# Both down products of a macaron encoder step by 7 products of half blocks

## The chip, the cores and the metric

One NeuronCore of a Trainium2 chip (trn2) runs one inference step of a streaming encoder in fp32 accuracy. The metric is the device time of an execution in microseconds.

## The reference

The kernel computes the whole layer for 16 meta tokens, 1024 prompt frames and 32 frames of a running stream (1072 tokens, 1024 channels). What the change touches is the half-step FFN at either end, with 2816 hidden channels:

```python
def half_ffn(x, g, w_gate, w_up, w_down):
    h = rmsnorm(x, g)
    return x + 0.5 * ((jax.nn.silu(h @ w_gate) * (h @ w_up)) @ w_down)

x = half_ffn(x, ffn1_norm[l], ffn1_w_gate[l], ffn1_w_up[l], ffn1_w_down[l])
h = rmsnorm(x, mix_norm[l])
... = jnp.split(h @ w_in[l], split_at, axis=-1)     # attention, HGRN2, gates, w_out
x = half_ffn(x, ffn2_norm[l], ffn2_w_gate[l], ffn2_w_up[l], ffn2_w_down[l])
y_prompt = rmsnorm(xp, final_norm)[:, N_META:]
```

FFN1 takes all 1072 tokens, FFN2 the 1056 without the meta tokens. Behind FFN1 the sums are normalised for the input projection; behind FFN2 they are normalised, transposed and written out.

## The kernel before, in words

Every fp32 matrix is held as two fp32r parts, `hi` (a copy rounded by ACT) and `lo` (the difference, made by DVE), both made by `split` (L202) or `weights` (L169); every product is three matmuls into one PSUM bank: hi by hi, hi by lo, lo by hi. Channels lie on the 128 partitions, tokens in the free dimension.

**The gate and up stage** (`Seven.unit`, L345) takes 256 hidden channels (two chunks of 128, a unit; 11 units, of which the first goes by `plain`) and the tokens in two halves `b` of two quarters each (`QW` = 268 columns in FFN1, `QW2` = 264 in FFN2). For each weight, gate then up, it forms sums S1 to S4 of half blocks on DVE and needs 7 products of half blocks for each `b` in place of 8; partial sums are kept in SBUF (`parts`) by ACT and added by DVE in `out`. `g` (silu(gate) times up) goes to `mid_dram` by the SP queue (`store`, L315).

**The down stage** (`Seven.down`, L421) is a plain product. It goes through 11 pairs of chunks: `prepare` loads and splits two 512 KB rows of the weight and two chunks of `mid_dram`; `multiply` takes three tiles of tokens (`TT`: 400, 384, 288; `TD`: 384, 384, 288), 8 output chunks and 2 x 3 matmuls each, in PSUM banks that rotate through all eight (`bank(rotate=True)`, L129), and DVE adds half of the sum to `acc` (L443), which was loaded with the residual. For the last two pairs PE's order is written out by hand (`PE.on`), so that `after` (the end of one tile) runs beside the products of the next.

- FFN1: `after1` writes `x1_dram` and calls `normalise` (L214): for each chunk ACT makes `xh` (L218) and DVE `xl` (L219), ACT the squares (L224, L227), POOL adds five of them and DVE three (L228); `finish` sums over the partitions on PE and takes the root. Then the input projection (`project_all`) begins with its weights.
- FFN2: `after2` takes the blocks of 128 tokens that are complete: 8 transposes into two banks, two squares with their sums on ACT (L1520), a root, a reciprocal, two scalings on DVE (L1528) and the write.

```python
for i, x in ((last - 1, 0), (last - 1, 1), (last, 0), (last - 1, 2), (last, 1), (last, 2)):
    multiply(i, *tiles[x])
    if i == last:
        after(*tiles[x])
```

## Time and profile before

| | us |
|---|---|
| runs | 2502.64, 2504.14, 2504.74 (median 2504.14) |
| profiled execution | 2504.92 |
| its span | 2503.1 |
| PE busy | 2449.8 (98%), 18972 matmuls |
| DVE, ACT, POOL busy | 1540.3 (62%), 891.9 (36%), 149.9 (6%) |
| DMA | 211.95 MB, 83 GB/s of HBM traffic over the span |

An engine's busy time is the sum over its instructions. Its share is an average over stages: gate and up of FFN1 end at 510.8 us, the first down product at 773.45; the second down product runs from 2226.8 to 2491.4. A wait of another engine matters only where PE, or the chain at the end, waits for it.

### The profile page before, as it was taken

The page shows a single profiled execution, that of the slowest core. Times are in us where ns is not written, and L with a number is a line of the kernel's source. Part 1 is how long each engine was busy: PE and PEld are TensorE (multiplying, and loading weights), DVE is VectorE, ACT ScalarE, POOL GpSimd, SP SyncE. Part 2 cuts the span into 40 slices and gives each one's busy share as a digit, 9 for nine tenths or more (in the row PEclk, how much of TensorE's full clock was granted, in tenths as well). Part 3 has the DMA queues.
Part 4 walks back from the last instruction along what each step waited for, and adds up shares of the span by engine and source line. Part 5 has one row for each costly group of instructions (what it writes and reads, how often), then busy time and mean ns, then how long its engine had stood idle before and what let it go on. Part 6 is the DMA issues. An engine that isn't in the chain of part 4 may idle for free. (4 is left out here: it accounts for less than half of the span.)

```text
span 2503.1 us, 46037 instructions
## 1 busy us (share of the span) xinstructions
PE 2449.8 (98%) x18972; PEld 2347.6 (94%) x18972; DVE 1540.3 (62%) x2862; ACT 891.9 (36%) x1783; POOL 149.9 (6%) x307
## 2 busy tenths in 40 slices
PE   6999999999999999999999999999899999999998
PEld 5999999999999998898888887999899999999998
DVE  5755555567776377764666665657855555557766
ACT  6433333421125233332454544323443333331112
POOL 1000000000003012121000000111000000000000
PEclk9999999999999999999999999999899999999999
DMA  7122222252313111111111222432222222253311
GB/s 202 56 87 71 88 71 88 79 201 95 104 43 114 51 44 48 56 52 50 52 44 44 56 61 79 170 108 82 92 78 69 86 78 77 92 184 103 100 57 77
DMA packets 231913, 211.95 MB, mean 85 GB/s; under 512 B 38214, under 2 KB 209478, under 8 KB 231702
## 3 DMA queue, kind: packets, MB, share of 16 engines
q1 hardware_dynamic: 231670, 209.00, 26.1%
q8 instruction: 149, 2.44, 0.4%
q14 instruction: 62, 0.51, 0.1%
q0 software_dynamic: 32, 0.00, 0.0%
HBM read 154.00 MB, written 54.97 MB: 83 GB/s over the span
## 5 line engine op out<-in xcount | busy, mean ns | idle before, releaser
L102 PE MATMUL ps_mm<-xh,whi 128*128 128x384 f32 (+2 forms) x952 | 317.8, 334 | 0.6 <-DVE raw L1194 0.6
L102 PE MATMUL ps_mm<-xh,wlo 128*128 128x384 f32 (+2 forms) x952 | 310.9, 327 | 0.0
L102 PE MATMUL ps_mm<-xl,whi 128*128 128x384 f32 (+2 forms) x952 | 310.6, 326 | 0.0
L186 ACT ACTIVATE whi<-raw 128x1024 fp32r<-128x1024 f32 x109 | 112.9, 1055 | 537.1 <-PE ps_z L102 346.3
L204 DVE TENSOR_TENSOR wlo<-raw,whi 128x1024 fp32r<-128x1024 f32 x80 | 76.7, 959 | 209.4 <-ACT whi L203 206.9
L102 PEld LDWEIGHTS ps_mm<-xh,whi 128*128 128x128 f32 x952 | 179.9, 189 | 9.1 <-issue 5.0
L443 DVE SCALAR_TENSOR_TENSOR acc<-ps_z,acc 128x384 f32<-128x384 f32 (+2 forms) x264 | 138.7, 525 | 71.5 <-PE ps_z L102 70.1
L102 PEld LDWEIGHTS ps_mm<-xl,whi 128*128 128x128 f32 x952 | 180.1, 189 | 1.1
L102 PEld LDWEIGHTS ps_mm<-xh,wlo 128*128 128x128 f32 x952 | 180.0, 189 | 0.4
L187 DVE TENSOR_TENSOR wlo<-raw,whi 128x1024 fp32r<-128x1024 f32 x109 | 133.1, 1238 | 26.7 <-ACT whi L186 24.4
L986 DVE TENSOR_TENSOR_SCAN left<-left,oneb 128x512 f32<-128x512 f32 (+6 forms) x112 | 107.4, 959 | 54.8 <-ACT left L118 54.3
L203 ACT ACTIVATE whi<-S 128x1024 fp32r<-128x1024 f32 x80 | 85.0, 1062 | 155.9 <-PE ps_z L102 145.2
L204 DVE TENSOR_TENSOR wlo<-S,whi 128x1024 fp32r<-128x1024 f32 x80 | 97.9, 1224 | 29.9 <-ACT whi L203 28.6
L102 PE MATMUL ps_z<-acc1s,whi 128*128 128x268 f32 (+1 forms) x480 | 106.0, 285 | 0.0
L102 PE MATMUL ps_z<-xl1s,whi 128*128 128x268 f32 (+1 forms) x368 | 105.1, 286 | 0.0
L102 PE MATMUL ps_z<-xh1s,wlo 128*128 128x268 f32 (+1 forms) x368 | 104.9, 285 | 0.0
L102 PE MATMUL ps_z<-xh1s,whi 128*128 128x268 f32 (+1 forms) x368 | 104.6, 284 | 0.0
L203 ACT ACTIVATE whi<-raw 128x1024 fp32r<-128x1024 f32 x80 | 67.7, 846 | 92.6 <-PE ps_z L102 92.6
L443 DVE SCALAR_TENSOR_TENSOR acc<-ps_mm,acc 128x384 f32<-128x384 f32 (+2 forms) x132 | 69.2, 524 | 35.8 <-PE ps_mm L102 33.8
L118 ACT ACTIVATE g<-g 128x268 f32<-128x268 f32 (+1 forms) x120 | 50.8, 423 | 87.3 <-DVE g L378 84.1
L102 PEld LDWEIGHTS ps_z<-acc1s,whi 128*128 128x128 f32 x480 | 80.0, 188 | 0.0
L988 DVE TENSOR_TENSOR aa<-aa,left 128x512 f32<-128x512 f32 (+6 forms) x112 | 61.5, 550 | 14.4 <-POOL left L982 0.5
(694 smaller groups left out, 7416.9 us busy)
## 6 DMA issues: line engine op xcount, KB each, us to landing
raw<-in_ffn_w_gate_dram SPq DMA_DIRECT2D x44, 512.0 KB, 3.6
raw<-in_ffn_w_up_dram SPq DMA_DIRECT2D x44, 512.0 KB, 3.6
raw<-in_ffn_w_down_dram SPq DMA_DIRECT2D x44, 512.0 KB, 4.2
raw<-in_w_in_dram SPq DMA_DIRECT2D x44, 512.0 KB, 3.7
mid_dram<-g SPq DMA_DIRECT2D x22, 536.0 KB, 2.7
g<-mid_dram SPq DMA_DIRECT2D x22, 536.0 KB, 3.6
mid_dram<-g SPq DMA_DIRECT2D x22, 528.0 KB, 2.7
g<-mid_dram SPq DMA_DIRECT2D x22, 528.0 KB, 4.1
```

Source lines behind the costliest of these rows:

```text
L102: return self.queue(nc.tensor.matmul(*args, **more))
L118: i = A.activation(out, in_, func, **more).ins
L186: A.activation(hi, raw, AF.Copy)
L187: V.tensor_tensor(lo, raw, hi.bitcast(F32), op=ALU.subtract)
L203: A.activation(dst_h, src, AF.Copy)
L204: V.tensor_tensor(dst_l, src, dst_h.bitcast(F32), op=ALU.subtract)
L443: V.scalar_tensor_tensor(acc[:, m, s], ps[:, :n], 0.5, acc[:, m, s], op0=ALU.mult, op1=ALU.add)
L986: V.tensor_tensor_scan(rev(st[:rows]), rev(st[:rows]), one, 1.0 if carry is None else carry[:rows], op0=ALU.mult, op1=ALU.mult)
L988: V.tensor_tensor(at[:rows, :n], at[:rows, :n], left[:rows, 513 - n:], op=ALU.mult)
```

## The change

The down products become products of half blocks too. A unit is 2 x 128 hidden channels; a position `mp` is 256 output channels; a half `b` is two quarters of tokens. For each of them 7 products stand in place of 8. The seven operands on the side of the tokens (`NAMES`) are formed in the gate stage, once per unit, as hi and lo, through two staging tiles (`st`, and the place of `R`), and are written to `mid_dram` by the POOL queue (`send`, one of them after every second step by `tick`). `home` reads them back on SP into the slots of `xh` and `xl` and extra places, three units in turn. `lanes` loads weights of two (unit, position) pairs, forms four sums of 256 columns and their hi and lo. A `Job` is a position with two lanes and both halves, in tiles of two PSUM banks (`pv`, two `pu`, `pf`); ACT copies the first product from `pv` to `pu` within PSUM, and DVE adds six results of 2 x 268 columns to `acc`, or ACT writes them where they are the first. p6 and p7 of a job run between p1 and p4 of the next. The last two units run half by half in tiles of one bank, and `after` follows each half, in PE's written order. `acc` is no longer loaded with the residual: it is added in eight pieces on the way (`add_residual`). In the last up unit the first half's seven products come before the second half's. `after1` takes the first 400 tokens after the first half, the other two tiles after the second; `after2` takes blocks 0 to 3, then 4 to 8, and its transposes use three banks.

```diff
-PLACES = ((0, 0, 0), (0, 0, 1), (1, 0, 0), (1, 0, 1), (1, 1, 0), (1, 1, 1), (0, 1, 0), (0, 1, 1))
+PLACES = ((0, 0, 0), (1, 0, 0), (1, 1, 0), (0, 1, 0), (0, 0, 1), (1, 0, 1), (1, 1, 1), (0, 1, 1))
+NAMES = ("B11", "T3", "B21", "T2", "T4", "T1", "B22")
...
+        def send(self, i, gs):
+            def part(c, th):
+                return gs[c][:, self.t0:].rearrange("p (b t n) -> p b t n", b=2, t=2)[:, :, th]
+            def away(name, v, left=None, right=None):
+                def work():
+                    if left is not None:
+                        V.tensor_tensor(v, left, right, op=ALU.subtract)
+                    x = NAMES.index(name)
+                    if x % 2:
+                        st = base.tile([P, 2, 2, self.qw], F32R, tag="R", name="st")
+                    else:
+                        st = self.pool.tile([P, 2, 2, self.qw], F32R, tag="st", name="st", bufs=1)
+                    split(st[:, 0], st[:, 1], v)
+                    nc.gpsimd.dma_start(self.mids[i, :, x], st.rearrange("p a b n -> p (a b) n").bitcast(F32))
+                self.later.append(work)
+            b11, b12, b21, b22 = (part(c, th) for c in range(2) for th in range(2))
+            away("B11", b11)
+            away("T1", b11, b12, b11)
+            away("B21", b21)
+            away("T3", b12, b22, b12)
+            away("B22", b22)
+            away("T2", b22, b22, b11)
+            away("T4", b21, b21, b22)
+        def tick(self):
+            self.groups += 1
+            if self.later and self.groups % 2:
+                self.later.pop(0)()
...
+            steps = first, second, third, fourth, fifth, sixth, seventh
+            if i == FC // 2 - 1 and not gate:
+                for b in range(2):
+                    for step in steps:
+                        step(b)
+            else:
+                for step in steps:
+                    for b in range(2):
+                        step(b)
+                    self.tick()
...
+        def home(self, i):
+            j = i % 3
+            tiles = [slots(tag, j, F32R, None, self.qw) for tag in ("xh", "xl")]
+            for tag, n in self.homes[j]:
+                tiles.append(self.pool.tile([P, 1, 4, self.qw], F32R, tag=tag, name=f"u_{tag}", bufs=n))
+            places = []
+            for t in tiles:
+                x, n = len(places), t.shape[1]
+                nc.sync.dma_start(t.bitcast(F32), self.mids[i, :, x:x + n])
+                places += [t[:, y] for y in range(n)]
+            return dict(zip(NAMES, places))
...
+            split(ah[:, 0], al[:, 0], a11)
+            split(ah[:, 1], al[:, 1], a12)
+            split(ah[:, 2], al[:, 2], a22)
+            s = self.tile("S", [P, 4, 2, P])
+            V.tensor_tensor(s[:, 2], a21, a22, op=ALU.add)
+            V.tensor_tensor(s[:, 1], s[:, 2], a11, op=ALU.subtract)
+            V.tensor_tensor(s[:, 0], a11, a21, op=ALU.subtract)
+            V.tensor_tensor(s[:, 3], a12, s[:, 1], op=ALU.subtract)
+            sh = wp.tile([P, 4, 2, P], F32R, tag="whi", name="whi")
+            sl = wp.tile([P, 4, 2, P], F32R, tag="wlo", name="wlo")
+            split(sh, sl, s)
...
+                def out(job, mh, th, ps):
+                    m = 2 * job.mp + mh
+                    if job.b is None:
+                        to = acc[m].rearrange("p (b t) n -> p b t n", b=2)[:, :, th]
+                    else:
+                        to = acc[m][:, 2 * job.b + th]
+                    if (m, th) in begun:
+                        V.scalar_tensor_tensor(to, job.at(ps), 0.5, to, op0=ALU.mult, op1=ALU.add)
+                    else:
+                        begun.add((m, th))
+                        A.activation(to, job.at(ps), AF.Copy, scale=0.5)
...
+                def p1(job):
+                    job.v = job.tile("pv")
+                    job.product(job.v, "A11", "B11", True)
+                    job.u = job.tile("pu")
+                    A.activation(job.at(job.u), job.at(job.v), AF.Copy)
+                def p2(job):
+                    job.f = job.tile("pf")
+                    job.product(job.f, "S3", "T3", True)
+                    job.out(1, 1, job.f)
+                def p3(job):
+                    job.product(job.v, "A12", "B21", False)
+                    job.out(0, 0, job.v)
+                def p4(job):
+                    job.product(job.u, "S2", "T2", False)
+                    job.out(1, 0, job.u)
+                def p5(job):
+                    job.product(job.f, "A22", "T4", False)
+                    job.out(1, 0, job.f)
+                def p6(job):
+                    job.product(job.u, "S1", "T1", False)
+                    job.out(1, 1, job.u)
+                def p7(job):
+                    job.product(job.u, "S4", "B22", False)
+                    job.out(0, 1, job.u)
+            def run(jobs):
+                before = None
+                for job in jobs:
+                    job.p1()
+                    if before:
+                        before.p6()
+                    job.p2()
+                    job.p3()
+                    if before:
+                        before.p7()
+                    job.p4()
+                    job.p5()
+                    before = job
+                before.p6()
+                before.p7()
...
+            def add_residual(m):
+                r = self.tile("s", [P, 4, qw])
+                nc.sync.dma_start(r.rearrange("p q n -> p (q n)"), resid[:, m, self.t0:])
+                V.tensor_tensor(acc[m], acc[m], r, op=ALU.add)
+            def steps():
+                units[0] = self.home(0)
+                W = self.lanes(w, ((0, 2), (0, 3)))
+                while self.later:
+                    self.later.pop(0)()
+                units[1] = self.home(1)
+                for l in range(2):
+                    yield Job(W, [(units[0], l)], 2 + l)
+                for s in range(1, last):
+                    for mp in ((0, 1) if s % 2 else (2, 3)):
+                        if mp % 2 == 0:
+                            units[s + 1] = self.home(s + 1)
+                        W = self.lanes(w, ((s - 1, mp), (s, mp)))
+                        if mp % 2 and s > 1:
+                            add_residual((s - 2) // 2 + (4 if s % 2 else 0))
+                        yield Job(W, [(units[s - 1], 0), (units[s], 1)], mp)
+            psum("pairs")
+            PE.on = True
+            run(steps())
+            psum("singles")
+            Ws = [self.lanes(w, ((last - 1, mp), (last, mp))) for mp in (2, 3)]
+            Ws.append(self.lanes(w, ((last, 0), (last, 1)),
+                                 [self.tile("raw2", [P, 3, 2, P], F32R) for _ in range(2)]))
             functions(final)
-            PE.on = True
-            for i, x in ((last - 1, 0), (last - 1, 1), (last, 0), (last - 1, 2), (last, 1), (last, 2)):
-                multiply(i, *tiles[x])
-                if i == last:
-                    after(*tiles[x])
-                elif x == 2:
-                    between()
+            for b in range(2):
+                jobs = [Job(Ws[x], [(units[last - 1], 0), (units[last], 1)], 2 + x, b) for x in range(2)]
+                jobs += [Job(Ws[2], [(units[last], l)], l, b) for l in range(2)]
+                run(jobs)
+                after(b)
+            between()
...
+        def after1(b):
+            if not fed:
+                fed.update(xh=big("xh", F32R), xl=big("xl", F32R), R=base.tile([P, T], F32, tag="R", name="R"))
+            flat = [a.rearrange("p q n -> p (q n)") for a in ff.acc]
+            for t0, n in TT[1:] if b else TT[:1]:
+                for m in range(KC):
+                    nc.sync.dma_start(x1_dram[:, m, t0:t0 + n], flat[m][:, t0:t0 + n])
+                normalise(pool, [a[:, t0:t0 + n] for a in flat], fed["xh"], fed["xl"], 1, fed["R"], t0, n)
...
-                    ps = bank(rotate=True)
+                    ps = bank(("mm", "mm", "tr")[rot[0] % 3])
+                    rot[0] += 1
                     for k in range(4):
-                        PE.transpose(ps[:r, k * P:(k + 1) * P], acc[:, 4 * hf + k, c0:c0 + r], ident)
+                        PE.transpose(ps[:r, k * P:(k + 1) * P], acc[4 * hf + k][:, c0 - N_META:c0 - N_META + r], ident)
                     A.activation(junk[:r], ps[:r], AF.Square, accum_out=ss[:r, hf:hf + 1])
```

The order of instructions at three places, before and after.

PE in FFN2, where the last two pairs of chunks are multiplied (before) and where the first half of the last two units ends (after). `cst` is the identity, `acc*` the sums that are transposed, `mid_*`, `whi`, `wlo` operands of the down product; a row `[waits DVE_49]` waits for DVE.

```order
L102 MATMUL ps_z<-mid_gb,raw_26076 128x384
L105 MATMUL ps_mm<-cst,acc_24091 128x128 [waits DMAHW1_49,DVE_49]
L105 MATMUL ps_mm<-cst,acc_24091 128x128 [waits DVE_49] x3
L105 MATMUL ps_z<-cst,acc_24091 128x128 [waits DVE_49] x4
L105 MATMUL ps_tr<-cst,acc_24091 128x128 x4
L105 MATMUL ps_z<-cst,acc_24091 128x128 x4
L105 MATMUL ps_o<-cst,acc_24091 128x128 x4
L105 MATMUL ps_z<-cst,acc_24091 128x128 x4
L102 MATMUL ps_mm<-mid_mh,whi 128x288 x2
L102 MATMUL ps_mm<-mid_mh,wlo 128x288
```

```order
L106 MATMUL ps_mm<-cst,acc1s 128x128 [waits DVE_49]
L106 MATMUL ps_mm<-cst,acc1s 128x128
L106 MATMUL ps_mm<-cst,acc2s 128x128 x2
L106 MATMUL ps_tr<-cst,acc0s 128x128 [waits DVE_49]
L106 MATMUL ps_tr<-cst,acc0s 128x128 x2
L106 MATMUL ps_tr<-cst,acc1s 128x128
L106 MATMUL ps_mm<-cst,acc1s 128x128 [waits DVE_49]
L106 MATMUL ps_mm<-cst,acc1s 128x128
L106 MATMUL ps_mm<-cst,acc2s 128x128 x2
L103 MATMUL ps_z<-xh0s,g 128x264 x3
L103 MATMUL ps_z<-xh1s,g 128x264 x3
```

Before, six transposed tiles follow each other in six banks and the products of the next tile come behind them. Now the tiles take `mm`, `mm` and `tr` in turn, each second half of a block waits for DVE, and the other half's first product stands behind all of them.

DVE at FFN1's end: `xl` is the low part of the projection's operand (three tensors by tile of tokens in the change), `acc*` the sums, `L443` and `L566` the results of products.

```order
L187 TENSOR_TENSOR wlo<-raw,whi 128x1024 [waits DMAHW0_49,Activation_49]
L443 SCALAR_TENSOR_TENSOR acc_5430<-ps_z,acc_5430 128x384 [waits PE_49]
L443 SCALAR_TENSOR_TENSOR acc_5430<-ps_o,acc_5430 128x384 [waits PE_49]
L219 SCALAR_TENSOR_TENSOR xl_5439<-acc_5430,gains,xh_5436 128x384 [waits Activation_49]
L443 SCALAR_TENSOR_TENSOR acc_5430<-ps_z,acc_5430 128x384 [waits PE_49]
L219 SCALAR_TENSOR_TENSOR xl_5439<-acc_5430,gains,xh_5436 128x384 [waits Activation_49]
L443 SCALAR_TENSOR_TENSOR acc_5430<-ps_mm,acc_5430 128x384 [waits PE_49]
L219 SCALAR_TENSOR_TENSOR xl_5439<-acc_5430,gains,xh_5436 128x384 [waits Activation_49]
L443 SCALAR_TENSOR_TENSOR acc_5430<-ps_z,acc_5430 128x384 [waits PE_49]
L219 SCALAR_TENSOR_TENSOR xl_5439<-acc_5430,gains,xh_5436 128x384 [waits Activation_49]
```

```order
L566 SCALAR_TENSOR_TENSOR acc2s<-ps_z,acc2s 128x268 [waits PE_49]
L566 SCALAR_TENSOR_TENSOR acc1s<-ps_z,acc1s 128x268 [waits PE_49]
L566 SCALAR_TENSOR_TENSOR acc2s<-ps_z,acc2s 128x268 [waits PE_49]
L566 SCALAR_TENSOR_TENSOR acc2s<-ps_o,acc2s 128x268 [waits DVE_49,PE_49]
L235 SCALAR_TENSOR_TENSOR xl_8259<-acc0s,gains,xh_8256 128x400 [waits PE_49,Activation_49]
L235 SCALAR_TENSOR_TENSOR xl_8259<-acc0s,gains,xh_8256 128x400 [waits Activation_49] x2
L235 SCALAR_TENSOR_TENSOR xl_8259<-acc1s,gains,xh_8256 128x400 [waits Activation_49] x3
L235 SCALAR_TENSOR_TENSOR xl_8259<-acc2s,gains,xh_8256 128x400 [waits Activation_49] x2
L566 SCALAR_TENSOR_TENSOR acc2s<-ps_z,acc2s 128x268 [waits PE_49]
L566 SCALAR_TENSOR_TENSOR acc0s<-ps_o,acc0s 128x268 [waits PE_49]
L566 SCALAR_TENSOR_TENSOR acc0s<-ps_z,acc0s 128x268 [waits PE_49]
L235 SCALAR_TENSOR_TENSOR xl_8261<-acc1s,gains,xh_8258 128x288 [waits Activation_49]
```

Before, one `xl` stands behind each result. Now the eight `xl` of the 400 tokens stand in a row between results of the second half; the first of them waits for PE, whose products read the same slot.

ACT where the down product of FFN1 begins: `pu<-pv` are the copies within PSUM, `acc*<-p*` first results of a position, `st<-g` the splits of operands that are sent to DRAM; `DMASW` is POOL's DMA queue.

```order
L186 ACTIVATE whi<-raw 128x1024 [waits DMAHW0_49,DVE_49,PE_49]
L186 ACTIVATE whi<-raw 128x1024 [waits DMAHW1_49,DVE_49,PE_49]
L203 ACTIVATE mid_xe_6104<-g 128x1072 [waits DMAHW6_49]
L203 ACTIVATE mid_s<-g 128x1072 [waits DMAHW7_49]
L186 ACTIVATE whi<-raw 128x1024 [waits DMAHW4_49,DVE_49,PE_49]
L186 ACTIVATE whi<-raw 128x1024 [waits DMAHW5_49,DVE_49,PE_49]
```

```order
L219 ACTIVATE st<-g 128x536 [waits DMASW7_49,DVE_49,Activation_49]
L219 ACTIVATE st<-g 128x536 [waits DMASW5_49,DVE_49]
L575 ACTIVATE pu<-pv 128x2x268 [waits PE_49,Activation_49]
L569 ACTIVATE acc1s<-pf 128x2x268 [waits PE_49]
L569 ACTIVATE acc1s<-pv 128x2x268 [waits PE_49]
L219 ACTIVATE whi<-S 128x1024 [waits DVE_49]
L569 ACTIVATE acc1s<-pu 128x2x268 [waits PE_49,Activation_49]
L575 ACTIVATE pu<-pv 128x2x268 [waits PE_49]
L219 ACTIVATE st<-g 128x536 [waits DMASW0_49]
L219 ACTIVATE st<-g 128x536 [waits DMASW1_49]
L569 ACTIVATE acc2s<-pf 128x2x268 [waits PE_49]
L569 ACTIVATE acc2s<-pv 128x2x268 [waits PE_49]
```

Before, ACT has only weights and `mid` tiles to split here. Now splits that wait for POOL's transfers stand between the copies and the results that PE's next products wait for.

## Rows read from the trace of the kernel before

**Rows 1.** The page's first part: the span, and each engine's busy time, its share of the span and its instructions.

```profile
span 2503.1 us, 46037 instructions
PE 2449.8 (98%) x18972; PEld 2347.6 (94%) x18972; DVE 1540.3 (62%) x2862; ACT 891.9 (36%) x1783; POOL 149.9 (6%) x307
```

**Rows 2.** Busy time by stretch of the span (us; in brackets the instructions): FFN1's gate and up stage, its down product (three), FFN2's gate and up stage, its down product (two), the end. The last columns are the granted TensorE clock, the busy share of the DMA engines and GB/s.

```profile
core 0: us, PE busy (x) PEld busy (x) DVE busy (x) ACT busy (x) POOL busy (x), PEclk, DMA share, GB/s
100.00:500.00 400.00, 400.00 (x3240) 400.00 (x3239) 210.44 (x342) 151.16 (x276) 0.00 (x0) 1.00 0.24 79
510.80:550.00 39.20, 39.20 (x232) 38.58 (x231) 26.41 (x45) 5.04 (x5) 0.00 (x0) 1.00 0.63 228
550.00:700.00 150.00, 150.00 (x923) 148.31 (x922) 105.99 (x178) 24.03 (x25) 0.00 (x0) 1.00 0.26 87
750.00:773.30 23.30, 23.30 (x154) 22.72 (x153) 22.84 (x41) 15.52 (x29) 11.19 (x10) 1.00 0.48 165
1800.00:2200.00 400.00, 400.00 (x3294) 400.00 (x3293) 214.23 (x348) 146.84 (x269) 0.00 (x0) 1.00 0.24 78
2226.80:2250.00 23.20, 23.20 (x146) 23.03 (x145) 14.23 (x26) 1.30 (x2) 0.00 (x0) 1.00 0.79 284
2250.00:2450.00 200.00, 199.26 (x1221) 195.93 (x1220) 144.42 (x240) 36.46 (x37) 0.00 (x0) 1.00 0.26 83
2491.40:2503.00 11.60, 2.81 (x26) 2.41 (x24) 5.66 (x14) 4.45 (x15) 0.00 (x0) 0.81 0.37 139
```

**Rows 3.** Where the two down products begin: the first PE group of each that reads a `mid` tile (minimum, median and maximum ns; first and last start within the window asked for).

```profile
L102 PE MATMUL ps_tr<-mid_xe,whi x6: 295/334/347, 510.8 to 528.3; 128*128 128x400 f32 x2, 128*128 128x384 f32 x2, 128*128 128x288 f32 x2
...
L102 PE MATMUL ps_mm<-mid_mh,whi x12: 290/337/339, 2226.8 to 2248.6; 128*128 128x384 f32 x8, 128*128 128x288 f32 x4
```

**Rows 4.** PE's timeline where the first down product ends and the input projection begins (start us, us, engine, line).

```profile
773.05 0.56 PE L102 MATMUL ps_tr<-mid_S,raw 128*128 128x288 f32 x3
773.45 0.34 PE L102 MATMUL ps_z<-xh,whi 128*128 128x400 f32 x1
```

**Rows 5.** DVE's groups from 100 to 773 us, each shape apart (busy us, mean ns of one | idle before).

```profile
L443 DVE SCALAR_TENSOR_TENSOR acc<-ps_z,acc 128x400 f32<-128x400 f32 x44 | 25.2, 572 | 3.2 <-PE ps_z L102 2.6
L204 DVE TENSOR_TENSOR mid_xe<-g,mid_xe 128x1072 fp32r<-128x1072 f32 x11 | 13.9, 1267 | 1.3 <-ACT mid_xe L203 1.3
L204 DVE TENSOR_TENSOR wlo<-raw,whi 128x512 fp32r<-128x512 f32 x20 | 13.9, 693 | 1.2
L378 DVE TENSOR_TENSOR g<-s,ps_z 128x268 f32<-128x268 f32 x30 | 13.0, 434 | 26.1 <-PE ps_z L102 21.1 <-ACT g L118 4.9
```

**Rows 6.** The same of ACT, from 100 to 800 us.

```profile
L203 ACT ACTIVATE whi<-raw 128x512 fp32r<-128x512 f32 x20 | 12.6, 632 | 28.3 <-PE ps_z L102 28.3
L391 ACT ACTIVATE s<-ps_z 128x268 f32<-128x268 f32 x19 | 7.5, 396 | 19.5 <-PE ps_z L102 19.4
L218 ACT ACTIVATE xh<-acc,gains 128x384 fp32r<-128x384 f32 x8 | 4.9, 614 | 1.4 <-DVE acc L443 1.4
```

**Rows 7.** DMA issues: out<-in, queue, count, KB each, median us from issue to landing.

```profile
mid_dram<-g SPq DMA_DIRECT2D x22, 536.0 KB, 2.7
gains<-in_ffn_norm_dram POOLq DMA_DIRECT2D x1, 4.0 KB, 5.3
gains<-in_mix_norm_dram SPq DMA_DIRECT2D x1, 4.0 KB, 6.1
```

**Rows 8.** FFN1's end on DVE, and POOL's adds there (timelines; x4 is four instructions in one row).

```profile
755.08 0.44 DVE L443 SCALAR_TENSOR_TENSOR acc<-ps_z,acc 128x288 f32<-128x288 f32 x1
755.44 0.44 DVE L443 SCALAR_TENSOR_TENSOR acc<-ps_o,acc 128x288 f32<-128x288 f32 x1
758.14 2.36 DVE L187 TENSOR_TENSOR wlo<-raw,whi 128x1024 fp32r<-128x1024 f32 x2
766.34 0.91 DVE L219 SCALAR_TENSOR_TENSOR xl<-acc,gains,xh 128x384 fp32r<-128x384 f32 x1
...
765.50 5.21 POOL L228 TENSOR_TENSOR t_tot<-t_tot,t_g 128x384 f32<-128x384 f32 x4
```

**Rows 9.** The end of the span, timeline of all engines: transposes (L105), squares with their sums (L1520), root, reciprocal and scaling (L1528) of the final blocks.

```profile
2491.42 0.60 PE L105 MATMUL ps_o<-cst,acc 128*128 128x128 f32 x4
2491.85 0.62 PE L105 MATMUL ps_z<-cst,acc 128*128 128x128 f32 x4
2492.77 0.60 ACT L1520 ACTIVATE t_junk<-ps_z 128x512 bf16<-128x512 f32 x1
2493.93 0.29 ACT L118 ACTIVATE rs<-rs,epsb 128x1 f32<-128x1 f32 x1
2494.52 0.75 DVE L1528 SCALAR_TENSOR_TENSOR yt<-ps_o,rs,gfin 128x512 f32<-128x512 f32 x1
2495.18 0.74 DVE L1528 SCALAR_TENSOR_TENSOR yt<-ps_z,rs,gfin 128x512 f32<-128x512 f32 x1
2498.84 0.73 DVE L1528 SCALAR_TENSOR_TENSOR yt<-ps_z,rs,gfin 32x512 f32<-32x512 f32 x1
```

165 lines of the change are left out of this document (92 added, 73 removed).

## The prediction

> **What bounds the kernel now.** I read the page's totals first. PE is busy 98% of the span, DVE 62%, ACT 36%, POOL 6% [rows 1]. Then busy time by stretch [rows 2]: PE is busy without a gap in both gate and up stages and in both down products, at granted clock 1.00, so there only fewer PE cycles can shorten anything, and any wait that the change brings shows in full. At the end of the span PE is busy for 2.81 of 11.60 us [rows 2]; there the chain of the final blocks counts. The profiled execution took 2504.92 us, 1.8 us more than its span and 0.8 us over the median of the three runs, 2504.14. The sum is made against 2504.9; 0.2% of it, 5 us, is about what a measurement of this kernel can tell from no change.
>
> **The products.** The first down product runs from 510.8 us [rows 3] to 773.45 us, where the input projection follows without a gap [rows 4]: 262.6 us for its 22 x 8 x 3 x 3 = 1584 matmuls. The second runs from 2226.8 [rows 3] to the last transposes at 2491.42 [rows 9]: 264.6 us, six blocks' transposes among it. After the change each is 11 units x 4 positions x 7 products x 2 halves x 3 = 1848 matmuls of 268 or 264 columns. That form is what the gate stages run: 400 us for 3240 is 0.1235 us each, 400 for 3294 is 0.1214 [rows 2]. So, if PE is always fed, 228.1 and 224.4 us: **34.5 and 40.2 us less**. All that follows is given back.
>
> **Inside the down stages** I cost the added work at nothing. A job (two lanes, one position) is 84 matmuls, 10.4 us. DVE takes six results of 2 x 268 columns, 0.71 us each along the line from 0.43 (268) to 0.57 (400), seven steps of 256 columns at about 0.42 (0.69 at 512), a `wlo` of 1.2 [rows 8] and, every second job, a residual addition of 1.27 [rows 5]: 9.0 us by durations, about 8 by starts, which lie 0.08 us closer than the durations (0.36 against 0.44 [rows 8]). ACT has some 3.5 us. Between a product and the next use of its two banks lie 24 to 36 other matmuls, 3.0 to 4.4 us; that covers a 0.7 us copy or result with its turn. If it does not, 36 jobs at up to 1 us each come on top.
>
> **Inside the gate stages** a unit is 336 matmuls, 41.5 us, and gets seven operands: seven splits of 536 columns (ACT about 0.65, DVE 0.71 [rows 5, 6]), four subtractions, seven writes of 549 KB. DVE goes from 0.53 to about 0.72 of the time, ACT from 0.38 to 0.49 [rows 2]; PE waits for neither, at nothing. But a split waits until the write before it left its staging tile, and partial sums in PSUM wait behind it on ACT and DVE. The trace has no such write on POOL's queue. The bounds are 2.7 us, the same bytes on SP's queue, and the 5.3 us of POOL's one 4 KB transfer plus 2.7, so 8 us [rows 7]. Each tile is taken every 11.8 us; with 1.4 us of splitting even 8 fits. I take 6. The Trainium skill (DMA: Bandwidth & Descriptors, Anatomy of one DMA) fits 2.0 us plus bytes/436e3 to such a transfer, an estimate of 3.3 us here; by it the next term would be 4 us less in all.
>
> **Gate to down, twice.** The last unit's seven operands are formed through the two staging tiles after its last products: four rounds on the first tile, each 1.4 us of splitting and 6 of writing. ACT's copies and results of the first jobs stand behind those splits, and the first unit's operands can land only after their slots are read for the last time. I follow some 2 us at the first copy, 1 to 2 us at each of two later ones: **5 us each**, between 1 and 12.
>
> **Pairs to singles, twice.** The banks are given over when the last two-bank results are out, and the four jobs of a half start and end with half the cover (6 matmuls, 0.74 us, against a copy of 0.40 [rows 6] with its turn): **3.3 us each**, between 1 and 6.
>
> **FFN1's end.** Before, each `xl` of DVE follows its result one by one [rows 8] and the projection's first two `wlo` were made at 758.14, 15 us ahead. After, in the second half, eight `xh` on ACT and eight `xl` on DVE wait for the slot of unit 9 and stand ahead of a PSUM copy and of results: 8 x 0.53 us (0.61 [rows 6] less the same 0.08) and what trails, with the squares ahead of them paced by POOL's 1.3 us additions (four took 5.21 [rows 8]): 8.5 us. After the last product eight `xh` of 384 wait for unit 10's slot (4.3 us), then come the squares paced by four POOL additions (to +10.5), two DVE additions, and only behind them the first `wlo` (1.2 us), 12.7 us after the last product; 16 projection matmuls (2.9 us) run before: 10 us idle. With 1.5 us for the last root and 2 for the sums that PE had before too, the end gives **22 us**, between 8 and 28. FFN1 is then 228.1 + 5 + 3.3 + 22 = 258.4, **4.2 us less**.
>
> **FFN2's end.** Before, transposes took any of eight banks in turn. Now they have three, so a block's second half waits for the scaling of the block before: from its transposes at 2491.85 over square, sum, root and reciprocal to the scaling's end at 2495.27, 3.4 us [rows 9]. Four blocks stand in PE's order between the halves: 0.5 + 3 x 3.4 + 0.6, with the late results, **12 us**; 2.5 us more for waits in the second half. The tail has five blocks: 0.5 + 4 x 3.4, then 3.4 + 0.7, 1 for the last results, 3.5 for the last write (from 2499.57, where the last scaling ends [rows 9], to 2503.1): **23 us** against 11.7. FFN2 is 224.4 + 5 + 3.3 + 12 + 2.5 + 23 = 270.2, against 276.3 before: **6.1 less**.
>
> After idle stretches the granted clock can fall; it did to 0.81 in the last 11.6 us [rows 2]. I add 2 us. Sum: 2504.9 - 4.2 - 6.1 + 2 = **2497**.
>
> **Rivals.**
> (A) The ends cost two thirds of what I follow, or less. My queue walk takes each wait at its full length; what speaks for less is that DVE and ACT have slack before it. Ends and transitions are 22 + 37.5 + 16.6 = 76 us; with 50 of them it is 2471. PE showing at most 4 us idle in FFN1's second half would mark it. Chance 0.26.
> (B) Slower: the down stages are bound by loading. A step of two jobs, 20.7 us, loads 3.84 MB of operands, 1.05 of weights and 0.55 of residual: 263 GB/s for 200 us. The highest rows show 228 and 284 GB/s, for 39 and 23 us, at shares of 0.63 and 0.79 [rows 2]. They speak against a limit below 284, but lasted a tenth of the time, and they were not loads into slots that are free only after their last use. If what is sustained is 245, a step takes 22.2 us; 9 steps twice add 27: 2524. It decides below 263. Chance 0.14.
> (C) Slower: POOL's writes land later than 10.4 us. At 12 a tile takes 13.4 instead of 11.8 us, 3.5 rounds a unit, 20 units: over 100 us more, about 2600. Against it: POOL's one transfer took no longer than SP's of the same size (5.3 against 6.1 us [rows 7]); for it: that was one transfer, and now there are 154 beside a DVE that is busy for 0.72 of the time. Chance 0.07. The Trainium skill (SBUF — State Buffer, SBUF: two separate sides) has a rule that would bring it: descriptors of a DMA from POOL's queue are written by GpSimd, which is locked out while DVE runs in a two-port mode. Whether DVE's operations here run so, no row shows.
> (D) Slower: the ends and transitions reach their upper bounds, or the 0.7 us results miss their cover by 0.3 us a job: 11 to 20 us more, 2508 to 2517. Chance 0.10.
> That the change doesn't do what it says is excluded by the order of PE's instructions.
>
> **How the numbers follow.** My sum has 0.43 for 2488 to 2510, cut by the bound at 2499.9: 0.25 under it, 0.18 within. Faster is that and A: 0.51. Slower by over 5 us is B, C, D: 0.31. The forecast's own range is 2488 to 2510. The range for 8 in 10 reaches from 2460 (half of A's savings more than its number, 0.07 left below) to 2530 (B and D within, C and a stronger B left out, 0.1 left above).
>
> **What would show it.** PE without gaps between 530 and 690 us at 810 matmuls per 100 us, and 260 GB/s there; gaps would be B or D by the waits ahead of them (DMA, or DVE). In the gate stages idle PE behind ACT's `st` splits would be C. At FFN1's end PE idle for 18 us in two pieces, behind a copy in PSUM and behind `wlo`. In FFN2 four blocks of transposes about 3.4 us apart between the halves, and the last write some 23 us after the last product. I am wrong if these ends take under 5 us each, or if PE waits in the middle of a down stage.

## The result and the profile after

| | us |
|---|---|
| runs of the change | 2514.53, 2516.30, 2517.13, 2517.87 (median 2516.72) |
| runs of the kernel before beside them | 2502.64 to 2505.37 (median 2504.44) |
| ratio | 1.0049, 95% interval 1.0031 to 1.0066 |
| profiled execution, its span | 2516.30, 2514.5 |

The change is slower by about 12 us: above the forecast's own range (2488 to 2510), inside its range for 8 in 10 (2460 to 2530), and on the other side of its sign. The page's first part and its rows of POOL's writes, of the change (compare [rows 1], [rows 7]):

```profile
span 2514.5 us, 47920 instructions
PE 2411.5 (96%) x19500; PEld 2303.7 (92%) x19500; DVE 1680.1 (67%) x3160; ACT 1019.9 (41%) x2113; POOL 230.9 (9%) x461
L349 POOL DMA_DIRECT2D mid_dram<-st x154 | 82.3, 534 | 904.4 <-DVE st L220 843.5
mid_dram<-st POOLq DMA_DIRECT2D x77, 536.0 KB, 3.8
```

PE's busy time fell by 38 us where the products need 75 less, in part because a matmul at the halved clock is busy for longer. Where PE is short of work shows by stretch (the columns are those of [rows 2]): FFN1's gates, its transition to the down product, the down product (two rows), its second half, the first projection; then FFN2's gates, transition, down product, the stretch that begins with the first half's transposes, the tail.

```profile
100.00:500.00 400.00, 399.07 (x3226) 398.64 (x3225) 279.45 (x459) 181.41 (x343) 35.72 (x67) 1.00 0.41 146
512.60:540.00 27.40, 20.00 (x131) 18.85 (x130) 14.89 (x25) 13.62 (x26) 3.20 (x6) 0.88 0.83 334
540.00:560.00 20.00, 20.00 (x164) 20.00 (x163) 13.78 (x27) 8.34 (x16) 0.00 (x0) 1.00 0.97 346
560.00:700.00 140.00, 139.35 (x1125) 138.62 (x1124) 110.51 (x196) 37.37 (x70) 0.00 (x0) 1.00 0.74 255
743.00:768.00 25.00, 20.00 (x129) 18.39 (x128) 18.55 (x42) 16.72 (x33) 3.15 (x3) 0.86 0.33 118
768.00:785.00 17.00, 8.08 (x33) 6.88 (x32) 12.53 (x16) 9.21 (x20) 9.93 (x9) 0.80 0.25 75
1800.00:2200.00 400.00, 400.00 (x3296) 400.00 (x3295) 281.62 (x456) 179.02 (x336) 36.34 (x68) 1.00 0.41 142
2229.40:2262.00 32.60, 24.74 (x165) 23.61 (x164) 17.34 (x32) 15.63 (x31) 3.20 (x6) 0.84 0.85 332
2262.00:2420.00 158.00, 156.31 (x1273) 155.13 (x1272) 121.40 (x220) 44.23 (x82) 0.00 (x0) 1.00 0.74 261
2459.50:2491.40 31.90, 24.52 (x160) 22.91 (x159) 16.86 (x40) 7.75 (x24) 0.00 (x0) 0.79 0.17 67
2491.40:2514.50 23.10, 7.78 (x42) 5.39 (x40) 9.06 (x21) 7.89 (x25) 0.00 (x0) 0.63 0.25 98
```

A stretch's length less its matmuls at full speed (0.1235 us each in FFN1, 0.1214 in FFN2) is what PE lost there; a few records are missing, so each such number holds to about 1 us. The gate stages and the inside of FFN1's down product lose next to nothing: 560 to 700 us has 1125 matmuls, 138.9 us of work. FFN2's down product loses 3.5 us of 158. The two transitions stand out: 131 matmuls in 27.4 us, 11.2 us lost, and 165 in 32.6, 12.6 us lost (the expectations below say 11.1 and 12.3, within that 1 us).

How far the change is ahead or behind at a place is read from one group of matmuls in both traces: the attention's first product with `aT`, and the first gate product of FFN2 (durations, then first and last start). Before, then the change:

```profile
L102 PE MATMUL ps_o<-aT,vt x720: 209/273/324, 1189.1 to 1530.3; 128*64 128x128 f32 x144, 128*64 128x32 f32 x32, 16*64 16x32 f32 x4
...
L102 PE MATMUL ps_mm<-xh0s,whi x16: 279/285/422, 1765.1 to 1798.2; 128*128 128x264 f32 x16
```

```profile
L103 PE MATMUL ps_o<-aT,vt x720: 209/273/324, 1194.4 to 1533.9; 128*64 128x128 f32 x144, 128*64 128x32 f32 x32, 16*64 16x32 f32 x4
...
L103 PE MATMUL ps_mm<-xh0s,whi x15: 279/283/422, 1767.1 to 1799.8; 128*128 128x264 f32 x15
```

FFN1 ends 5.3 us late (forecast: 4.2 early); the mixer behind it, which the change leaves alone, gives 3.3 of that back; FFN2 adds 9.4 to the span (forecast: 6.1 less).

**The transition, step by step.** ACT's timeline in the change where FFN1's gate stage ends (the bracket is its idle time before, and what ended it):

```profile
516.96 1.19 ACT L219 ACTIVATE st<-g 128x536 fp32r<-128x536 f32 x2 [4.66 <-DMA mid_dram<-st]
518.05 0.60 ACT L575 ACTIVATE pu<-pv 128x536 f32<-128x536 f32 x1
...
527.52 0.65 ACT L219 ACTIVATE st<-g 128x536 fp32r<-128x536 f32 x1 [2.45 <-DMA mid_dram<-st]
530.14 0.65 ACT L219 ACTIVATE st<-g 128x536 fp32r<-128x536 f32 x1 [1.97 <-DMA mid_dram<-st]
```

POOL's timeline, where the writes are issued:

```profile
506.82 0.53 POOL L349 DMA_DIRECT2D mid_dram<-st  x1 [19.65 <-DVE st L220]
518.65 1.16 POOL L349 DMA_DIRECT2D mid_dram<-st  x2 [11.29 <-DVE st L220]
```

PE's timeline there, only rows ahead of which it was idle:

```profile
514.03 1.00 PE L103 MATMUL pv<-xh0s,g 128*128 128x268 f32 x6 [1.29 <-DVE g L432]
518.70 1.71 PE L103 MATMUL pv<-xh0s,g 128*128 128x268 f32 x6 [2.93 <-ACT pu L575]
529.60 0.52 PE L103 MATMUL pu<-u_xe,whi 128*128 128x268 f32 x2 [2.86 <-DVE acc1s L566]
532.66 0.85 PE L103 MATMUL pv<-xh0s,g 128*128 128x268 f32 x3 [0.31 <-ACT g L219]
```

Read together: the first job's copy `pu<-pv` stands on ACT behind a split into `st`, which waits until the write before it has left that tile. That write was issued at 506.82 and done at about 516.9. In the gate stage a write lands after 3.8 us (2.9 to 5.8 from 100 to 500 us). In the transition, beside loads of the next units, the first three of the seven land after 10.0, 8.8 and 10.8 us, which is when ACT's splits at 516.96, 527.52 and 530.14 begin; the last four take 3.0 to 4.3. PE waits for the copy, and eleven microseconds later for a result on DVE that stands behind the next such split. PE's first wait, 1.29 us, is another: the last result of the gate stage on DVE (`g`). FFN2's transition repeats all three (1.32, 3.64 and 2.90 us), with first writes of 10.7, 8.5 and 10.6 us.

### The profile page after: what moved, and what is told of

Its sections match the earlier page's. It is cut to its first block, busy times and chain, and to the rows that moved or that the text cites. A ratio compares the mean times of both kernels' runs of the same rounds, so it can differ in the third digit from the quotient of the medians.

```text
span 2514.5 us, 47920 instructions
## 1 busy us (share of the span) xinstructions
PE 2411.5 (96%) x19500; PEld 2303.7 (92%) x19500; DVE 1680.1 (67%) x3160; ACT 1019.9 (41%) x2113; POOL 230.9 (9%) x461
## 4 chain that ended last, share of the span: by engine, by line
PE 54%; issue 31%; DVE 7%; POOL 3%; DMA 3%; ACT 2%; SPq 0%; POOLq 0%; DVEq 0%; ACTq 0%
PE ps_mm L103 20%; PE ps_z L103 12%; PE pu L103 6%; PE ps_o L103 5%; PE pf L103 4%; PE pv L103 4%; POOL mid_dram L349 3%; PE ps_tr L103 2%; PE ps_tr L106 2%; DMA mid_dram<-st 1%; DMA raw<-in_ffn_w_down_dram 1%; PE ps_z L106 1%; PE ps_mm L106 1%; DVE wlo L203 1%; DVE xl L235 0%
## 5 line engine op out<-in xcount | busy, mean ns | idle before, releaser
L219 ACT ACTIVATE whi<-S 128x1024 fp32r<-128x1024 f32 x124 | 131.4, 1060 | 311.3 <-PE pu L103 157.8
L220 DVE TENSOR_TENSOR wlo<-S,whi 128x1024 fp32r<-128x1024 f32 x124 | 151.7, 1223 | 37.5 <-ACT whi L219 34.8
L220 DVE TENSOR_TENSOR st<-g,st 128x536 fp32r<-128x536 f32 (+1 forms) x154 | 107.6, 709 | 101.2 <-ACT st L219 100.8
L349 POOL DMA_DIRECT2D mid_dram<-st x154 | 82.3, 534 | 904.4 <-DVE st L220 843.5
L202 ACT ACTIVATE whi<-raw 128x1024 fp32r<-128x1024 f32 x67 | 70.5, 1057 | 175.9 <-PE ps_mm L103 136.3
L219 ACT ACTIVATE st<-g 128x536 fp32r<-128x536 f32 (+1 forms) x154 | 96.9, 642 | 88.4 <-DMA mid_dram<-st 75.1
L220 DVE TENSOR_TENSOR wlo<-raw,whi 128x1024 fp32r<-128x1024 f32 x80 | 76.6, 958 | 73.2 <-ACT whi L219 71.5
L103 PE MATMUL ps_z<-xh2s,whi 128*128 128x268 f32 (+1 forms) x352 | 100.3, 285 | 0.9 <-ACT s L454 0.9
L103 PE MATMUL ps_z<-xl2s,whi 128*128 128x268 f32 (+1 forms) x352 | 100.3, 285 | 0.0
L103 PE MATMUL ps_z<-xh2s,wlo 128*128 128x268 f32 (+1 forms) x352 | 100.1, 285 | 0.0
L203 DVE TENSOR_TENSOR wlo<-raw,whi 128x1024 fp32r<-128x1024 f32 x67 | 83.2, 1246 | 25.3 <-ACT whi L202 25.1
```

Of the source, the lines that this page charges most:

```text
L103: return self.queue(nc.tensor.matmul(*args, **more))
L202: A.activation(hi, raw, AF.Copy)
L203: V.tensor_tensor(lo, raw, hi.bitcast(F32), op=ALU.subtract)
L219: A.activation(dst_h, src, AF.Copy)
L220: V.tensor_tensor(dst_l, src, dst_h.bitcast(F32), op=ALU.subtract)
L349: nc.gpsimd.dma_start(self.mids[i, :, x], st.rearrange("p a b n -> p (a b) n").bitcast(F32))
```

## The experiments

Ratios are to the kernel before, run on the same chip beside them; the change itself is 1.0049.

| run | median us | ratio (95%) | span of the profile |
|---|---|---|---|
| nolast | 2495.14 | 0.9967 (0.9954 to 0.9979) | 2493.7 |
| sync | 2515.39 | 1.0052 (1.0037 to 1.0067) | 2514.7 |
| spread | 2518.45 | 1.0058 (1.0043 to 1.0073) | 2516.7 |
| gforms | 2523.88 | 1.0088 (1.0073 to 1.0103) | 2521.7 |
| late | 2512.65 | 1.0029 (1.0017 to 1.0041) | 2510.7 |
| late2 | 2507.05 | 1.0018 (1.0009 to 1.0027) | 2505.9 |
| ust | 2518.00 | 1.0053 (1.0036 to 1.0070) | 2516.4 |
| earlyw | 2511.32 | 1.0037 (1.0024 to 1.0049) | 2507.6 |
| late1 | 2516.86 | 1.0059 (1.0044 to 1.0074) | 2515.9 |
| banks | 2505.86 | 1.0009 (0.9999 to 1.0018) | 2504.3 |
| inter | 2505.20 | 1.0004 (0.9994 to 1.0013) | 2502.1 |
| ie | 2501.47 | 0.9991 (0.9981 to 1.0000) | 2499.8 |
| best3 | 2494.00 | 0.9960 (0.9945 to 0.9975) | 2492.6 |
| best4 | 2490.14 | 0.9948 (0.9933 to 0.9963) | 2491.0 |

**nolast: is it the last unit's operands?** They are neither formed nor written, and unit 10's products read unit 9's.

```diff
-                nc.sync.dma_start(t.bitcast(F32), self.mids[i, :, x:x + n])
+                nc.sync.dma_start(t.bitcast(F32), self.mids[min(i, FC // 2 - 2), :, x:x + n])
...
-                while self.later:
-                    self.later.pop(0)()
+                self.later.clear()
```

> The seven operands of the last unit are not formed or written in either FFN (the loads that would read them read the unit before; its output is left wrong by that part). If the 11.1 and 12.3 us lost at the two gate to down changes come from ACT and DVE standing behind splits that wait for POOL's writes, they fall to 1 to 3 us each, with the halved clock: 17 to 20 us less, near 2498. If PE waits there for the first units' operands, whose loads fill the DMA engines, the loss stays over 6 us each and the time over 2506.

Busy time by stretch (columns as above):

```profile
512.60:540.00 27.40, 26.12 (x211) 25.70 (x210) 14.89 (x31) 15.28 (x29) 0.00 (x0) 1.00 0.74 296
```

211 matmuls in place of 131, at a granted clock of 1.00; what is left is 1.3 us of idle PE in each transition, behind the last `g`. So the seven operands cost 21 us of the span. But two things are gone together: the splits in ACT's and DVE's order, and 3.8 MB of writes. The next runs take them apart.

**sync: is it POOL's queue?** The writes are issued on SP's queue.

```diff
-                    nc.gpsimd.dma_start(self.mids[i, :, x], st...)
+                    nc.sync.dma_start(self.mids[i, :, x], st...)
```

> The 154 operand writes go out on SP's queue in place of POOL's; nothing else. If they land late at the gate to down changes because loads of the first units fill the DMA engines, the first one there still takes 8 to 11 us, the loss stays 10 to 13 us each and the time within 4 us of the changed kernel. If POOL's queue itself is what makes them late, they land in about 3 us there and the loss falls by 4 us or more each, to below 2508.

No gain, though neither side of the expectation came out. Over all writes the page gives landings of 3.8 and 4.3 us. In FFN1's transition the first write takes 6.6 us and the next two 2.7 and 4.1 (the two after them have no recorded landing), where POOL's took 10.0, 8.8 and 10.8. PE gets through 189 matmuls in place of 131, and then waits for a weight. Busy time by stretch, and PE's row:

```profile
512.60:540.00 27.40, 24.58 (x189) 23.57 (x190) 15.35 (x27) 15.73 (x29) 0.00 (x0) 1.00 0.90 341
```

```profile
548.41 0.51 PE L103 MATMUL pv<-xh1s,g 128*128 128x268 f32 x2 [3.41 <-ACT g L219]
```

The loads and weights on SP now stand behind the writes, so the wait has moved (4.55 us at 2270.02 in FFN2). The run changes the queue and what stands ahead of the loads at once, so it does not tell whether POOL's queue has a part in the late writes. In the change the DMA engines were busy for 0.98 of the time from 518.6 to 530.1, while two late writes were under way; in sync for 0.77 from 515 to 520.

**spread: fewer splits ahead of the first job.** Two operands are formed ahead of it, the others between the jobs; the third unit is loaded one job later, and the next pair's weights go to tiles of their own.

```diff
-                while self.later:
-                    self.later.pop(0)()
...
+                form(2)
...
+                    form(l)
...
+                form(2)
...
+                        if s == 1 and mp == 1:
+                            form(2)
```

> The same seven operands are formed, but two before the first job, one before the second, two each before the third and fourth, and the second unit's successor is loaded one job later. If only the waiting in ACT's queue costs, most of what the kernel without these operands gains stays: 10 to 16 us less than the changed kernel, near 2503. If the writes land late because loads fill the DMA engines for 30 us, splits still wait and 3 to 6 us come back.

No gain, and the trace shows that the order did not change where it matters: the scheduler that sets ACT's order still put the waiting split ahead of the copy (518.08, idle for 5.11 us behind `mid_dram<-st`; the copy at 519.17).

**gforms: take the splits off ACT and DVE.** GpSimd forms five of the seven operands, and the next pair's weights go to tiles of their own.

```diff
...
-                    split(st[:, 0], st[:, 1], v)
+                    if own:
+                        G.tensor_copy(st[:, 0], v)
+                        G.tensor_tensor(st[:, 1], v, st[:, 0].bitcast(F32), op=ALU.subtract)
+                    else:
+                        split(st[:, 0], st[:, 1], v)
```

> Five of the last unit's seven operands are formed by GpSimd (copy and subtractions), off ACT's and DVE's queues; the third weight pair takes other tiles, since the unit's own stay in use longer. If ACT's and DVE's order is what costs, the loss of 11.1 and 12.3 us falls to 2 to 5 each (GpSimd needs some 20 us, and the fourth weight pair waits for the tiles it frees): 14 us less, near 2503. If the tiles are freed too late the loss moves to a wait for weights and stays over 9 each.

Worse, for a reason that no theory held: the operands are formed from `g`, and the weights of a later step take those same tiles. On ACT:

```profile
537.08 1.03 ACT L219 ACTIVATE g<-raw 128x256 fp32r<-128x256 f32 x3 [12.54 <-POOL st L352]
```

ACT stands there for 12.54 us, and PE for 10.38 us behind the copy that follows. A late reader moved the wait to whoever writes next.

**late: no split ahead of a copy waits for a write.** Four operands go through four different tiles before the first job; the other three are tied behind its products, so that the scheduler cannot put them earlier. The next pair's weights go to tiles of their own.

```diff
+                    if i == FC // 2 - 1 and name in ("B21", "T3", "T4"):
+                        st = self.tile("s", [P, 2, 2, self.qw], F32R)
...
+                    if i == FC // 2 - 1 and name in ("B22", "T2", "T4"):
+                        made = A.activation(st[:, 0], v, AF.Copy).ins
+                        tc.add_manual_dep(made, mark[0].name, order, reason="late")
...
```

> Of the last unit's seven operands of each FFN, four (B11, T1, B21, T3, in four different tiles) are formed before the first job, as none of them waits for a write; the other three (B22, T2, T4) stand behind the first job's products. If the transitions cost 11 to 12 us because ACT's and DVE's queues hold splits that wait for writes, ahead of PSUM copies and results that PE waits for, the two transitions (11.1 and 12.3 us lost) fall to 2 to 4 us each: 2516.7 - 16 = about 2500, between 2497 and 2504. If it is the loading (385 to 435 GB/s at a busy share of 0.95 to 0.99) that holds PE, by landings of the first operands and weights, nothing is gained: 2515 to 2518, and PE's longest waits end with a DMA or with the weights' splits.

Between the two: 4 to 5 us of the 16 (by the medians, by the ratios). The waits of the first job are gone, and another stands 20 us later. PE, then DVE, then SP's queue:

```profile
515.50 1.01 PE L103 MATMUL pv<-xh0s,g 128*128 128x268 f32 x6 [1.30 <-DVE g L439]
522.92 0.52 PE L103 MATMUL pu<-u_xe,whi 128*128 128x268 f32 x2 [0.15 <-DVE acc1s L573]
...
543.86 0.52 PE L103 MATMUL pu<-u_xe,whi 128*128 128x268 f32 x2 [3.69 <-DVE acc0s L573]
```

```profile
542.75 0.42 DVE L528 TENSOR_TENSOR S<-raw 128x256 f32<-128x256 f32 x1 [7.64 <-DMA raw<-in_ffn_w_down_dram]
543.10 0.71 DVE L573 SCALAR_TENSOR_TENSOR acc0s<-pu,acc0s 128x536 f32<-128x536 f32 x1
```

```profile
515.14 0.93 SPq L504 DMA_DIRECT2D u_xe<-mid_dram  x2
535.68 0.32 SPq L504 DMA_DIRECT2D u_st<-mid_dram  x1
536.05 1.01 SPq L514 DMA_DIRECT2D raw<-in_ffn_w_down_dram  x2
```

PE waits for a result; the result stands on DVE behind the forming of a weight; the weight `raw` stands on SP behind the load of `u_st`, which has to wait for the last write from the tile `st`. SP issued nothing for 20 us. In the change the same pair stands at 538.61 and 539.03, but PE was late by then.

**late2 and ust: the load that holds SP.** `u_st` of the third unit goes to POOL's queue, on top of late (late2) and alone (ust).

```diff
-                nc.sync.dma_start(t.bitcast(F32), self.mids[i, :, x:x + n])
+                queue = nc.gpsimd if i == 2 and x == len(NAMES) - 1 else nc.sync
+                queue.dma_start(t.bitcast(F32), self.mids[i, :, x:x + n])
```

> The kernel 'late' with one load moved: the third unit's last operand (u_st, which waits for the last write from the staging tile) is issued by POOL's queue, so that the weights of the next pair no longer stand behind it on SP's queue. In 'late' PE was idle there for 3.69 and 4.33 us behind DVE, which stood at a weight (raw, issued at 536.05, 0.4 us after u_st, landed at 542.75) with a result behind it. If that order on SP is the second half of the transitions' cost, both gaps and the halved clock behind them go, 5 us each: 2512.7 - 10 = about 2503, with PE idle 1.3 us in each transition. If the transfers themselves are the bound (0.99 busy from 515 to 540), the weights land as late, or the operands do, and nothing is gained: 2511 to 2514.

> The same move of the one load (u_st to POOL's queue) in the kernel as changed, nothing else. If the splits that wait for writes come first and hide the weights' lateness (PE had no gap behind a weight there), nothing is gained: 2515 to 2518. If SP's order alone makes the transitions dear, it falls by 10 us or more.

Alone it gives nothing, as expected. On top of late it gives 3 to 6 of the 10 us (by the ratios, by the medians). `raw` is issued 19 us earlier and needs three times as long. The issue on SP, ACT behind its landing, and busy time by stretch, of late2:

```profile
516.70 0.39 SPq L515 DMA_DIRECT2D raw<-in_ffn_w_down_dram  x1
```

```profile
538.83 0.42 ACT L219 ACTIVATE g<-raw 128x256 fp32r<-128x256 f32 x1 [4.47 <-DMA raw<-in_ffn_w_down_dram]
539.15 0.60 ACT L583 ACTIVATE pu<-pv 128x536 f32<-128x536 f32 x1
```

```profile
510.00:545.00 35.00, 32.86 (x257) 31.69 (x256) 23.14 (x43) 20.31 (x36) 3.73 (x7) 1.00 1.01 400
```

22.1 us from issue to landing for 512 KB, with all DMA engines busy for 35 us at 400 GB/s. The transfers themselves are what these rows leave as the limit: the transition has three units of operands to load and one to write in some 45 us. The granted clock stays at 1.00 there. That is rival B's mechanism, in a place where the forecast had not looked for it. The Trainium skill (DMA: Bandwidth & Descriptors, Specifications) lists 435 GB/s for the fabric and about 358 for the HBM of one core; the 400 measured here lies above the second.

**earlyw and late1: FFN1's end.** In the change PE is idle twice there:

```profile
758.57 0.81 PE L103 MATMUL ps_z<-u_xe,whi 128*128 128x268 f32 x2 [3.02 <-DVE acc2s L566]
...
777.66 0.70 PE L103 MATMUL ps_z<-xh,wlo 128*128 128x400 f32 x1 [8.92 <-DVE wlo L203]
```

earlyw splits the projection's first two weights ahead of the last two tiles' normalisation; late1 normalises the first 400 tokens only behind the second half.

```diff
+            if b:
+                for h in range(2):
+                    col = COL_ZF + h * P
+                    made[col] = weights([(w_in[0][:, col:col + P], KC)], ...)
```

```diff
-            for t0, n in TT[1:] if b else TT[:1]:
+            for t0, n in TT if b else ():
```

> Only FFN1's end: the weights of the input projection's first two units are split ahead of the last two tiles' normalisation, in tiles that the down product has left. If PE's 8.9 us there are the wait of the first low weights behind that normalisation, they fall to 1 to 2 us, and with the halved clock behind them 8 to 9 us go; of FFN1's 5.2 us that are late only 1.8 were still late before FFN2's down product, so 3 to 8 us of the whole: near 2510. If the projection then waits for something else of the normalisation, nothing comes back.

> Only FFN1's end: the first 400 tokens are normalised after the second half, like the others, in place of beside it. If the 9.0 us lost in the second half come from the normalisation standing among PSUM copies and results on ACT and DVE, they fall to 1 to 2 us, and the wait behind the last product grows from 8.9 to some 18 us, since eight xh, eight xl and eight squares more come first: 0 to 5 us slower than the changed kernel. If the second half's loss is of the half-length jobs themselves, it stays near 9 and the time is 8 us or more slower.

With earlyw the 8.92 us become 3.14, behind the sums of POOL; the run is 3 to 5 us shorter (by the ratios, by the medians). With late1 PE's idle time in the second half falls from 5.0 to 1.5 us, and that behind the last product grows to 14.84. So the work of the normalisation is on the path wherever it stands; only its order against the weights can be had.

**banks and inter: FFN2's middle.** banks lets the blocks' transposes take all eight banks in turn, as before the change; a part of the last sums is then left out of its output, for a reason that no run here shows. inter puts one early block behind each of the second half's four jobs.

```diff
-                    ps = bank(("mm", "mm", "tr")[rot[0] % 3])
-                    rot[0] += 1
+                    ps = bank(rotate=True)
```

```diff
+                def among():
+                    for job in jobs:
+                        yield job
+                        if b == 1 and hasattr(after, "one"):
+                            after.one()
+                run(among())
...
```

> Only the transposes behind FFN2 are changed: they take the eight banks in turn, as before the change, in place of three. If the three banks make the 13.0 us between the halves and part of the 23.1 us tail, the four blocks there cost PE about 4 us and the tail about 14: 18 us less, and some 2 us less of halved clock, so near 2497 us (ratio 0.992 to the changed kernel). If instead the chain of squares, roots and scalings on ACT and DVE sets the pace whatever the banks, blocks stay 2.5 us or more apart, PE still does not wait between the halves but the tail gives back 4 us at most: near 2502.

> The three banks stay; the four blocks of the first half are put one by one behind the four jobs of the second half, in PE's written order. If the cost is that PE's order holds four waiting blocks in a row, the 13.0 us fall to about 3 and the halved clock after them goes: 10 to 12 us less, near 2506; the tail stays at 23 us. If ACT and DVE are what is short there, each block now delays the results of the job beside it and less than 5 us come back.

PE's rows ahead of which it was idle, in the change (four blocks between the halves) and in banks:

```profile
2463.60 0.69 PE L106 MATMUL ps_tr<-cst,acc1s 128*128 128x128 f32 x2 [2.58 <-DVE yt L1729]
...
2467.62 0.69 PE L106 MATMUL ps_mm<-cst,acc1s 128*128 128x128 f32 x2 [2.06 <-DVE yt L1729]
...
2471.65 0.69 PE L106 MATMUL ps_mm<-cst,acc1s 128*128 128x128 f32 x2 [2.06 <-DVE yt L1729]
```

```profile
2464.65 0.63 PE L103 MATMUL ps_z<-xh0s,g 128*128 128x264 f32 x3 [1.05 <-DVE yt L1728]
2470.57 0.81 PE L103 MATMUL ps_o<-xh0s,whi 128*128 128x264 f32 x2 [4.92 <-DVE yt L1728]
```

With eight banks the transposes follow each other without a wait, in 3.5 us, and the next products then wait for a bank that a scaling still reads. So most of the 10 us gained lies in the tail, 15.3 us from its first transpose at 2489.02 in place of 23.1; the expectation had 18 in all. With inter no block waits at all between the halves: 11 us gained, at the same tail.

**ie, best3, best4: the repairs together.** ie is inter with earlyw, best3 adds late, best4 the moved load.

> FFN2's four early blocks one by one behind the four jobs of the second half, and the projection's first two weights ahead of the last two tiles' normalisation at FFN1's end. They are 1,700 us apart; if what they gained alone (11.5 and 5.4 us) is time on PE's path at two places, the sum is 2516.7 - 16.9 = about 2500. If the second gives back later what the first one took, as the mixer gave back 3.3 us of FFN1's delay in the change, it is 2503 to 2506.

> All three repairs at once: four operands of the last unit ahead and three behind the first job, the early blocks one by one, the projection's weights first. If the three causes are separate, the sum is 2516.7 - 16 - 11.5 - 5.4 = about 2484, faster than the kernel before by some 19 us: what the seven products save (34.5 + 40.2) less the ends that stay. If the loading holds the transitions, it is about 2500.

> 'best3' with the same load moved. If the two waits of the transitions (splits behind writes, weights behind u_st) are all that they lose, 2494.0 - 10 = about 2484; if the transfers bound them, 2494.

inter and earlyw add up: 15 us, where their sum by medians is 16.9. best3 is at 2494.0, 10 above its forecast, as late alone had already missed. best4 is the fastest kernel here, 0.52% under the kernel before (interval 0.37 to 0.67%); the DMA engines stay busy throughout the transition, as in late2:

```profile
512.00:545.00 33.00, 29.02 (x227) 27.86 (x225) 20.27 (x38) 16.85 (x31) 3.73 (x7) 1.00 1.02 406
```

## Why the prediction was wrong

Against the profiled execution the forecast was 7.9 us less and 11.4 more was measured, a miss of 19.3. By its own steps:

- **Products, and the inside of the stages: right.** 1125 matmuls in 140 us in FFN1's down product, at 255 GB/s, so rival B does not hold there; it would have shown gaps. FFN2's product lost 3.5 us from 2262 to 2420 where the step had none.
- **Gate stages: nearly right.** No loss inside, at 0.70 of DVE and 0.45 of ACT (forecast 0.72 and 0.49). A write lands after 3.8 us where 6 was taken. The estimate of the Trainium skill (DMA: Bandwidth & Descriptors, Anatomy of one DMA), 3.3 us, was nearer. PE leaves the gate stages 1.8 us late in FFN1 and 0.6 in FFN2 (2229.4 against 2226.8, of which 2.0 came from before): 2.4 us not in the sum.
- **Gate to down, and the allowance for the clock: the step that failed.** 5 us each were taken; 11.2 and 12.6 were lost: 13.8 of the 19.3 us, the second above the bound of 12. The place and the mechanism were named (copies on ACT behind splits that wait for a write). The size was wrong in two terms.
  - The waits: of the 23.8 us, PE's idle time is 15.3 where the step's walk along the queues had 10. 2.6 of it is the wait for the last `g`, which the walk left out. The rest stands behind the first three writes, which took 8.5 to 10.8 us where the walk took 6 for each. The mean of a transition's seven writes, 6.2 and 6.5 us, is near that 6, but the slow ones come first, ahead of the copies.
  - The clock: the other 8.5 us passed with PE at work, in stretches with a granted clock of 0.88 and 0.84. In nolast, without these waits, it is 1.00. The sum had one allowance of 2 us for the whole kernel.
- **Pairs to singles: right.** 4.1 and 4.2 us (700 to 743 and 2420 to 2459.5 us, 315 and 291 matmuls) for 3.3.
- **FFN1's end: right in place, its first number in part by luck.** 9.0 us lost in the second half (forecast 8.5), 8.92 idle behind the last product (forecast 10), at places that the step named: results on DVE behind the eight `xl`, and `wlo`. But in the second half PE is idle for only 5.0 us, and the rest went with the clock, 0.86 there, for which the step had nothing; the 18 us of idle time that were to show it are 13.9.
- **FFN2's end: right within 2 us, in part by luck.** Transposes from 2459.55 to 2472.42, 12.9 us for 12, then 3.5 for 2.5, of which only 0.7 is waiting; the blocks are 4.0 us apart where 3.4 was taken, at a granted clock of 0.79 over that stretch and 0.63 in the tail. The tail is 23.1 us for 23, but by two errors that cancel: its transposes take 16.6 us for 14.1, what follows them 6.5 for 8.6.
- **The mixer: not looked at.** It gave back 3.3 us of FFN1's delay. No run here says how.

Rival D, "ends and transitions at their upper bounds" (2508 to 2517), is what happened, at the transitions alone; it had 0.10. Rival C did not come: no write took longer than 5.8 us in the gate stages. The rule of the Trainium skill (SBUF — State Buffer, SBUF: two separate sides), that DVE in a two-port mode holds up the descriptors of POOL's queue, did not show in the gate stages: with DVE busy for 0.70 a write landed after 3.8 us on POOL's queue. For the transitions, where writes on SP's queue landed sooner (sync), no run here decides it; the DMA engines were busy there.

What the runs show of the transitions' 23.8 us: without the operands of the last unit 21 us of the span are gone (nolast); an order in which no waiting split precedes a copy gives 4 to 5 (late); one load off SP's queue 3 to 6 more (late2); and what then stays goes with a DMA that is busy throughout. That this last part is the transfers' limit is read from late2's rows (22.1 us for 512 KB) and from nolast, which has 3.8 MB less to move; a run that takes only bytes away and leaves the order was not made. Nor does a run tell POOL's queue from the order of the loads. The part that the halved clock adds, 8.5 us, is what is left of the loss when the idle time is taken off; no run measured it by itself.

## What to carry to other kernels

Read the price of a transfer in the stretch where it will stand, not in the stage that happens to show it: a write of half a megabyte took 3.8 us beside light loads and 10 us where the next stage's loads begin. Give each wait the clock that it costs as well: here 15.3 us of idle PE cost 23.8. Where a stage ends by handing its products over through DRAM, sum the bytes that both sides move there before any wait is priced, and look for every in-order queue on which something that waits for those bytes stands ahead of work that PE needs: there were three here, ACT's, DVE's and SP's, one behind the other. Taking one such wait away shows the next, so a saving is only counted when the run shows PE fed.
